# One f32 stack of two experts in place of two split ones, and a weight ring that grows once the dense experts are done

## The chip, the cores and the metric

The kernel runs on one core of a Trainium2 chip. The metric is device time in microseconds (us), lower is better. One execution is profiled; the times that follow from several runs are given beside it.

## The reference

A decoder layer for 256 tokens of width 2048: a token mixer (latent attention and an mLSTM, merged by gates), and then a mixture of 32 experts of width 512. Each token picks one group of eight experts and two experts in it. Only the second part is touched by the change:

```python
g_sel = jnp.argmax(g_logits, axis=-1)                      # one group of 4
top_p, top_i = lax.top_k(jax.nn.softmax(e_in, axis=-1), TOP_K)   # two experts of its 8
weights = g_w[:, None] * top_p / jnp.sum(top_p, axis=-1, keepdims=True)
comb = jnp.sum(jax.nn.one_hot(expert_idx, N_EXPERTS) * weights[..., None], axis=1)
...
hg = jnp.einsum('td,edf->tef', t, w_gate_e[sl])
hu = jnp.einsum('td,edf->tef', t, w_up_e[sl])
act = jax.nn.silu(hg) * hu * comb[:, sl, None]
out = out + jnp.einsum('tef,efd->td', act, w_down_e[sl])
```

An expert's weights are 12 MiB in f32. The reference multiplies every expert with every token and weights most products by zero; the kernel needs only the tokens that chose an expert. The reference's router, evaluated on the drawn inputs (seed 0), gives expert 0 133 tokens, and the others, sorted, 139, 50, 23, 19, 19, 17, 16, 13 and fewer; five experts get none.

## The kernel before

Up to about 780 us the kernel runs the mixer. From there on it runs the experts, and the rest of this text is about them.

**Units of work.** A router on the chip counts the tokens of each expert and ranks the experts by it. Expert 0 is taken out (`static`) and computed as a *dense* expert, for all 256 tokens, without waiting for the router; so is rank 0 (`HEAVY`). Ranks 1 and 2 are a *stack of one* each (`("stack", 1, 1)`): up to 128 tokens are gathered into the columns of one operand. Ranks 3 to 26 are six *stacks of four* (`LIGHT`): 32 columns each, so that four experts' tokens lie side by side in the 128 columns. Ranks 27 to 30 (`LAST`) run only if rank 27 has tokens. An expert with more tokens than its columns hold (`cap`, L1186 to L1188) goes through a loop at the end (`spill`) as a dense expert.

**Precision and cost.** Dense experts and stacks of one split each weight slab of 1 MiB into two parts, `whi` and `wlo` (`split`: ScalarE copies, VectorE subtracts), and multiply three times in fp32r (`mm3`, `mm_wide`). Stacks of four use the f32 slab as it lies in the ring (L1298, L1346), four matmuls of 32 columns for each 128 rows of weights, each on its own quarter of TensorE's columns.

**Buffers.** 1 MiB buffers come from two pools: `u8` (9) and `v8` (4, two of which hold the token rows `xr`). A ring of `RING = 7` of the `u8` serves the stacks of four (`fetch_used`, which skips the load of a rank without tokens); the `v8` two serve the split experts (`fetch`, "rawb" in the trace). `split` has three `whi` and three `wlo` of half that size (`W4 = 3`).

**What sets the order.** SyncE issues every load, in the order of the program. A load into the ring waits until TensorE has read what lay there; a load into a `v8` buffer waits until VectorE has split what lay there; whatever stands behind a waiting load waits too. The program itself is written by two generators, `heavy` and `light`, that are asked in turn: the one whose share of its total is behind goes next (`done[0] / total[0] > done[1] / total[1]`). A dense slab half counts 0.5, a chunk of a stack (one slab of each of its experts) counts its number of experts. `HEAVY_RATE = 1.8` sets the heavy total, 86.4 against 288 for the light one. On TensorE, ScalarE and VectorE a scheduler then orders the instructions, and each engine runs them strictly in that order.

Of the kernel before, what the change touches and what calls it, by code (L numbers as in the profile page):

```python
# [9 lines left out]
F32 = mybir.dt.float32  # L10
F32R = mybir.dt.float32r
# [7 lines left out]
P = 128  # L19
# [19 lines left out]
HTURN = [1, 1]  # L39
HEAVY_RATE = 1.8  # L40
W4 = 3
# [25 lines left out]
DENSE = 0  # L67
HEAVY = [("dense", 0), ("stack", 1, 1), ("stack", 2, 1)]
LIGHT = [("stack", r, 4) for r in (3, 7, 11, 15, 19, 23)]
LAST = ("stack", 27, 4)  # L70
# [3 lines left out]
def decoder_layer_kernel(ctx, tc, xT, c, pos, cols_d, const_d, mask_d, w_ada, w_head, w_half, w_blk, w_mlv, w_pa, w_pb, w_out,  # L74
# [14 lines left out]
    def u8(name, dt=F32):  # L89
        return big.tile([P, 2048], dt, name=name, tag="u8")  # L90

    def flat(x):
# [786 lines left out]

    def load_expert(e, w, ch, rank=None):  # L880
# [3 lines left out]
        src = w[bass.ds(e, 1), ch].rearrange("a p k -> p (a k)")  # L884
        return fetch(src) if rank is None else fetch_used(src, rank)

# [155 lines left out]
    def s2(name, dt=F32):  # L1042
        return b2.tile([P, 512], dt, name=name, tag="t2b")
# [45 lines left out]
    def router():  # L1089
# [132 lines left out]

    def halves(raw):
        return [split(raw[:, i * 1024:(i + 1) * 1024]) for i in range(2)]

    def prep(r0, E, heavy):
        C = P // E
# [17 lines left out]
        vec.tensor_scalar(gT[:, :T], cb[:, :T], 0.0, None, op0=ALU.is_gt)  # L1245
        xg = [u8("xg")] if E > 1 else [[], []]
        for q in range(4):
            b = bank("xb")
            for i in range(4):
                k = 4 * q + i  # L1250
                for tt in range(2):
                    pe.matmul(b[:, i * P:(i + 1) * P], xr[tt][:, k * P:(k + 1) * P], gt[tt], start=tt == 0, stop=tt == 1)  # L1252
            dst = xg[0][:, q * 512:(q + 1) * 512] if E > 1 else s2("xf")
# [6 lines left out]
            if E == 1:  # L1260
                hi, lo = tx("xh", "txh", F32R)[:, :512], tx("xl", "txl", F32R)[:, :512]
                act.activation(hi, dst, AF.Copy)
                vec.tensor_tensor(lo, dst, hi.bitcast(F32), op=ALU.subtract)
                xg[0].append(hi)
                xg[1].append(lo)
        return xg, gT, wc

    def mm_wide(out, xh, xl, wh, wl, first, last):
        pe.matmul(out, xh, wh, start=first, stop=False)
        pe.matmul(out, xl, wh, start=False, stop=False)  # L1270
        pe.matmul(out, xh, wl, start=False, stop=last)

    pre = {}

    def stack(r0, E, last):
# [4 lines left out]

        def gu_chunks():
            for m in range(8):
                ch = 4 * (m % 2) + m // 2
                raws = [load_expert(expert(n), w_gu, ch, n if E > 1 else None) for n in ranks]
                for a in range(2):
                    yield ch // 4, 4 * (ch % 4) + 2 * a, ([split(raws[0][:, a * 1024:(a + 1) * 1024])] if E == 1 else
                                                          [r[:, a * 1024:(a + 1) * 1024] for r in raws])

        for u, k0, ws in ahead1(gu_chunks()) if E == 1 else gu_chunks():
            for k in (k0, k0 + 1):  # L1290
                us = slice((k - k0) * 512, (k - k0 + 1) * 512)
                if E == 1:
                    ks = slice((k % 4) * P, (k % 4 + 1) * P)
                    mm_wide(gu[u], xg[0][k // 4][:, ks], xg[1][k // 4][:, ks], ws[0][0][:, us], ws[0][1][:, us],
                            k == 0, k == KT - 1)
                else:
                    for j in range(E):
                        pe.matmul(gu[u][j * C:(j + 1) * C, :], xg[0][:, k * P + j * C:k * P + (j + 1) * C], ws[j][:, us],  # L1298
                                  start=k == 0, stop=k == KT - 1)
            yield 0.5 * E  # L1300
        s = s2("s")
# [4 lines left out]
        for f in range(4):  # L1306
            pe.transpose(ab[:, f * P:(f + 1) * P], s[:, f * P:(f + 1) * P], ident)
        aT = [s2("aT", F32 if E > 1 else F32R) for _ in range(1 if E > 1 else 2)]
        act.activation(aT[0], ab, AF.Copy)
        if E == 1:  # L1310
            vec.tensor_tensor(aT[1], ab, aT[0].bitcast(F32), op=ALU.subtract)

        def dn_chunks():
            for ch in range(4):
                raws = [load_expert(expert(n), w_dn, ch, n if E > 1 else None) for n in ranks]
                yield ch, ([halves(raws[0])] if E == 1 else raws)

# [17 lines left out]
        done = None  # L1335
        for ch, ws in dn_chunks():
            yb = bank("yb")
            for f in range(4):
                fs = slice(f * P, (f + 1) * P)
                if E == 1:  # L1340
                    wh, wl = ws[0][f // 2]
                    o = slice((f % 2) * 512, (f % 2 + 1) * 512)
                    mm_wide(yb, aT[0][:, fs], aT[1][:, fs], wh[:, o], wl[:, o], f == 0, f == 3)
                else:
                    for j in range(E):
                        pe.matmul(yb[j * C:(j + 1) * C, :], aT[0][:, f * P + j * C:f * P + (j + 1) * C],  # L1346
                                  ws[j][:, f * 512:(f + 1) * 512], start=f == 0, stop=f == 3)
# [23 lines left out]


    def unit(u):
# [5 lines left out]
    def stream(units, gen=None):  # L1379
        heavy = gen is not None  # L1380
        ready = lambda u: u[0] == "dense" or u[1] in pre
        for i in range(-1 if gen else 0, len(units)):
            if i >= 0:
                if not ready(units[i]):
                    pre[units[i][1]] = prep(*units[i][1:], heavy)
                gen = unit(units[i])
            for what in gen:
                if what != "act":
                    yield what
                else:  # L1390
                    if i + 1 < len(units) and not ready(units[i + 1]):
                        pre[units[i + 1][1]] = prep(*units[i + 1][1:], heavy)
# [175 lines left out]
```

## Time and profile before

| | us |
|---|---|
| median of 3 runs (lowest to highest) | 1686.77 (1675.19 to 1690.32) |
| the profiled execution | 1683.75 |
| its span in the trace | 1682.0 |
| TensorE busy in the span | 1501.5 (89%) |
| VectorE, ScalarE busy | 895.5, 562.3 |
| bytes moved, mean rate | 561.02 MB, 334 GB/s |
| mean granted clock | 0.963 |

The share of busy time is a mean over stages with different limits, so the views by stretch are the ones to read: which engine is busy throughout, and at what rate the loads run beside it. A matmul's duration in the trace is longer than the distance to the next one, since they are pipelined; the distance between two starts is its cost. An f32 matmul is two records, so a row of "x2" is one of them. The trace's "idle before" names what ended a wait.

### The profile page before, as it was taken

The page shows a single profiled execution, that of the slowest core. Times are in us where ns is not written, and L with a number is a line of the kernel's source. Part 1 is how long each engine was busy: PE and PEld are TensorE (multiplying, and loading weights), DVE is VectorE, ACT ScalarE, POOL GpSimd, SP SyncE. Part 2 cuts the span into 40 slices and gives each one's busy share as a digit, 9 for nine tenths or more (in the row PEclk, how much of TensorE's full clock was granted, in tenths as well). Part 3 has the DMA queues.
Part 4 walks back from the last instruction along what each step waited for, and adds up shares of the span by engine and source line. Part 5 has one row for each costly group of instructions (what it writes and reads, how often), then busy time and mean ns, then how long its engine had stood idle before and what let it go on. Part 6 is the DMA issues. An engine that isn't in the chain of part 4 may idle for free.

```text
span 1682.0 us, 25284 instructions
## 1 busy us (share of the span) xinstructions
PE 1501.5 (89%) x9924; PEld 1071.2 (64%) x9924; DVE 895.5 (53%) x1272; ACT 562.3 (33%) x790; POOL 88.0 (5%) x91
## 2 busy tenths in 40 slices
PE   8799999999999999999978999988988887768775
PEld 5698997999999999999636565644443333113212
DVE  5877799888776789976313334444443421102102
ACT  3134665446645664444303122222322211001000
POOL 0140013000000000220000000000000000000000
PEclk9899999999999999999989999999999989999989
DMA  8978668888676789864679889779999999999997
GB/s 344 395 286 327 260 234 292 317 286 289 245 259 240 269 339 375 329 254 160 262 316 388 343 368 389 308 322 421 412 421 393 403 416 397 406 410 385 405 388 287
DMA packets 78467, 561.02 MB, mean 334 GB/s; under 512 B 8705, under 2 KB 8961, under 8 KB 11905
## 3 DMA queue, kind: packets, MB, share of 16 engines
q1 hardware_dynamic: 78050, 558.84, 84.3%
q8 instruction: 82, 1.34, 0.3%
q10 hardware_dynamic: 288, 0.45, 0.1%
q14 instruction: 47, 0.39, 0.1%
HBM read 569.74 MB, written 2.10 MB: 340 GB/s over the span
## 4 chain that ended last, share of the span: by engine, by line
PE 69%; DMA 18%; DVE 7%; ACT 3%; issue 2%; POOL 0%; SPq 0%; DVEq 0%; POOLq 0%; ACTq 0%
PE gu L1298 12%; DMA ring<-in_w_gu_dram 10%; DMA ring<-in_w_dn_dram 6%; PE yb L1346 5%; PE ga L196 4%; PE ga L198 4%; PE xb L1252 3%; PE ga L197 3%; DVE wlo L184 2%; DVE raw L140 2%; PE hp L198 2%; PE hp L196 2%; PE hp L197 2%; PE gu L196 2%; PE gu L198 2%
## 5 line engine op out<-in xcount | busy, mean ns | idle before, releaser
L1298 PE MATMUL gu<-ring,xg 128*32 128x512 f32 x1536 | 295.0, 672 | 74.1 <-DMA ring<-in_w_gu_dram 74.1
L183 ACT ACTIVATE whi<-raw 128x1024 fp32r<-128x1024 f32 (+1 forms) x222 | 229.8, 1039 | 272.5 <-PE ga L197 82.0
L184 DVE TENSOR_TENSOR wlo<-raw,whi 128x1024 fp32r<-128x1024 f32 (+1 forms) x222 | 267.4, 1211 | 85.0 <-ACT whi L183 83.3
L140 DVE SCALAR_TENSOR_TENSOR raw<-raw,cond 128x2048 f32<-128x2048 f32 x96 | 220.0, 2294 | 19.5 <-DMA raw<-in_w_ada_dram 19.4
L1298 PEld LDWEIGHTS gu<-ring,xg 128*32 128x32 f32 x1536 | 61.6, 120 | 248.2 <-DMA ring<-in_w_gu_dram 131.9
L184 DVE TENSOR_TENSOR wlo<-rawb,whi 128x1024 fp32r<-128x1024 f32 x84 | 99.5, 1222 | 131.4 <-ACT whi L183 131.4
L1346 PE MATMUL yb<-ring,aT 128*32 128x512 f32 x768 | 130.8, 604 | 21.7 <-DMA ring<-in_w_dn_dram 18.9
L196 PE MATMUL ga<-hh,whi 128*128 128x256 f32 x512 | 149.9, 293 | 0.0
L198 PE MATMUL ga<-hh,wlo 128*128 128x256 f32 x512 | 145.3, 284 | 0.8 <-DVE wlo L184 0.8
L197 PE MATMUL ga<-hl,whi 128*128 128x256 f32 x512 | 145.1, 283 | 0.0
L183 ACT ACTIVATE whi<-rawb 128x1024 fp32r<-128x1024 f32 x84 | 84.7, 1050 | 118.7 <-DMA rawb<-in_w_dn_dram 43.9
L1321 DVE TENSOR_TENSOR yl<-yb,yh 128x512 fp32r<-128x512 f32 x32 | 22.1, 690 | 155.4 <-ACT yh L1320 155.4
L196 PEld LDWEIGHTS ga<-hh,whi 128*128 128x128 f32 x512 | 98.0, 191 | 5.2 <-issue 3.8
L1320 ACT ACTIVATE yh<-yb 128x512 fp32r<-128x512 f32 x32 | 19.1, 597 | 242.9 <-PE yb L1346 216.0
L198 PEld LDWEIGHTS ga<-hh,wlo 128*128 128x128 f32 x512 | 98.0, 191 | 1.3 <-DVE wlo L184 1.2
L197 PEld LDWEIGHTS ga<-hl,whi 128*128 128x128 f32 x512 | 98.1, 192 | 0.8 <-issue 0.7
L198 PE MATMUL hp<-hh,wlo 128*128 128x256 f32 x320 | 91.8, 287 | 3.4 <-DVE wlo L184 3.2
L196 PE MATMUL hp<-hh,whi 128*128 128x256 f32 x320 | 92.8, 290 | 0.0
L197 PE MATMUL hp<-hl,whi 128*128 128x256 f32 x320 | 91.2, 285 | 0.0
L1346 PEld LDWEIGHTS yb<-ring,aT 128*32 128x32 f32 x768 | 29.5, 110 | 92.4 <-issue 46.7
L1302 ACT ACTIVATE s<-gu 128x512 f32<-128x512 f32 x8 | 4.8, 596 | 216.7 <-PE gu L1298 212.5
L196 PE MATMUL gu<-xgh,whi 128*128 128x258 f32 x256 | 73.8, 292 | 3.3 <-ACT whi L183 3.3
(435 smaller groups left out, 3105.8 us busy)
## 6 DMA issues: line engine op xcount, KB each, us to landing
ring<-in_w_gu_dram SPq DMA_DIRECT2D x192, 1024.0 KB, 10.1
raw<-in_w_ada_dram SPq DMA_DIRECT2D x96, 1024.0 KB, 6.7
ring<-in_w_dn_dram SPq DMA_DIRECT2D x96, 1024.0 KB, 10.4
raw<-in_w_blk_dram SPq DMA_DIRECT2D x32, 1024.0 KB, 5.0
rawb<-in_w_gu_dram SPq DMA_DIRECT2D x26, 1024.0 KB, 8.8
raw<-in_w_half_dram SPq DMA_DIRECT2D x20, 1024.0 KB, 6.3
raw<-in_w_out_dram SPq DMA_DIRECT2D x16, 1024.0 KB, 6.0
rawb<-in_w_dn_dram SPq DMA_DIRECT2D x16, 1024.0 KB, 9.4
```

Source lines behind the costliest of these rows:

```text
L140: vec.scalar_tensor_tensor(raw, raw, 1.0, cond, op0=ALU.mult, op1=ALU.mult, accum_out=mod[:, i:i + 1])
L183: keep(act.activation(hi, raw, AF.Copy))
L184: keep(vec.tensor_tensor(lo, raw, hi.bitcast(F32), op=ALU.subtract))
L196: pe.matmul(out, wh, xh, start=first, stop=False)
L197: pe.matmul(out, wh, xl, start=False, stop=False)
L198: pe.matmul(out, wl, xh, start=False, stop=last)
L1252: pe.matmul(b[:, i * P:(i + 1) * P], xr[tt][:, k * P:(k + 1) * P], gt[tt], start=tt == 0, stop=tt == 1)
L1298: pe.matmul(gu[u][j * C:(j + 1) * C, :], xg[0][:, k * P + j * C:k * P + (j + 1) * C], ws[j][:, us], start=k == 0, stop=k == KT - 1)
L1302: act.activation(s, gu[0], AF.Silu)
L1320: act.activation(yh, yb, AF.Copy)
L1321: vec.tensor_tensor(yl, yb, yh.bitcast(F32), op=ALU.subtract)
L1346: pe.matmul(yb[j * C:(j + 1) * C, :], aT[0][:, f * P + j * C:f * P + (j + 1) * C], ws[j][:, f * 512:(f + 1) * 512], start=f == 0, stop=f == 3)
```

## The change

Four things change.

1. Ranks 1 and 2 leave `HEAVY` and become one stack of two, the first unit of `LIGHT`: 64 columns for each expert, f32 slabs from the ring, two matmuls for each 128 rows of weights, nothing split. `cap` follows: 64 tokens for ranks 1 and 2. The code for stacks of one is gone.
2. The heavy total becomes `HEAVY_SHARE = 0.2` of the light total: 62.4 against 312.
3. The first group of matmuls of each chunk is kept together: the matmul of the last expert is issued first and the others after it (`together`), so no matmul of a chunk runs before the chunk's last slab has landed.
4. `whi` and `wlo` become halves of one 1 MiB tile (`w8`, three of them). When the heavy stream is through, the ring takes over two `v8` and three `w8`, one per chunk, and has 12 buffers.

```diff
-HEAVY_RATE = 1.8
+HEAVY_SHARE = 0.2
...
-HEAVY = [("dense", 0), ("stack", 1, 1), ("stack", 2, 1)]
-LIGHT = [("stack", r, 4) for r in (3, 7, 11, 15, 19, 23)]
+HEAVY = [("dense", 0)]
+LIGHT = [("stack", 1, 2)] + [("stack", r, 4) for r in (3, 7, 11, 15, 19, 23)]
...
-        hi = w4.tile([P, 1024], F32R, name="whi", tag="whi")[:, :n]
-        lo = w4.tile([P, 1024], F32R, name="wlo", tag="wlo")[:, :n]
+        both = w8("whl", F32R)
+        hi, lo = both[:, :n], both[:, 1024:1024 + n]
...
+    room = [u8] * RING
+
     def fetch_used(src, rank):
-        if len(ring) < RING:
-            ring.append(u8("ring"))
+        if room:
+            ring.append(room.pop(0)("ring"))
             nc.sync.dma_start(ring[-1], src)
             return ring[-1]
...
-        vec.tensor_scalar(cap, rank, 3.0, 96.0, op0=ALU.is_lt, op1=ALU.mult)
-        vec.tensor_scalar(over[:, 1:2], rank, 1.0, 128.0, op0=ALU.is_lt, op1=ALU.mult)
+        vec.tensor_scalar(cap, rank, 3.0, 32.0, op0=ALU.is_lt, op1=ALU.mult)
+        vec.tensor_scalar(over[:, 1:2], rank, 1.0, 192.0, op0=ALU.is_lt, op1=ALU.mult)
...
+    def together(calls):
+        head = calls[-1]()
+        with tc.issue_after(head.ins):
+            for call in calls[:-1]:
+                call()
...
+        def packed(out, x, k, ws, cut, first, stop):
+            def one(j):
+                return lambda: pe.matmul(out[j * C:(j + 1) * C, :], x[:, k * P + j * C:k * P + (j + 1) * C], ws[j][:, cut],
+                                         start=first, stop=stop)
+            return [one(j) for j in range(E)]
+
+        for m in range(8):
+            ch = 4 * (m % 2) + m // 2
+            u, k0 = ch // 4, 4 * (ch % 4)
+            ws = [fetch_used(expert_slab(n, w_gu, ch), n) for n in ranks]
...
+            together(calls[0])
+            for group in calls[1:]:
+                for call in group:
+                    call()
+            yield E
...
-    n_heavy, n_light = 12.0 * (1 + sum(u[2] if len(u) > 2 else 1 for u in HEAVY)) * HEAVY_RATE, 12.0 * sum(u[2] for u in LIGHT)
+    n_light = 12.0 * sum(u[2] for u in LIGHT)
+    n_heavy = HEAVY_SHARE * n_light
...
-    forced = []
+    forced, later = [], [v8] * 2 + [w8] * W4
...
             done[i] += got
+            if not streams[0] and later:
+                room.append(later.pop(0))
```

How it moves instructions shows at two places. The first is TensorE's order where the first chunk of the first stack meets the dense expert (`gu_7597` to `gu_7599` before, `gu_7387` to `gu_7389` now, are the dense expert's banks; `ring_...` is a slab of a stack). Before, a single matmul of the chunk stands between dense ones:

```order
L197 MATMUL gu_7597<-xgl_7234,whi_8051 128x258
L1298 MATMUL gu_7901<-ring_7912,xg_7848 32x512
L198 MATMUL gu_7597<-xgh_7233,wlo_8052 128x258
L196 MATMUL gu_7598<-xgh_7233,whi_8051 128x258
L197 MATMUL gu_7598<-xgl_7234,whi_8051 128x258
L198 MATMUL gu_7598<-xgh_7233,wlo_8052 128x258
```

Now the whole chunk stands in one piece:

```order
L199 MATMUL gu_7389<-xgh_7175,whl_7884 128x258
L1285 MATMUL gu_7688<-ring_7710,xg_7635 64x512
L1285 MATMUL gu_7688<-ring_7699,xg_7635 64x512 x2
L1285 MATMUL gu_7688<-ring_7710,xg_7635 64x512
L1285 MATMUL gu_7688<-ring_7699,xg_7635 64x512
...
L200 MATMUL gu_7389<-xgl_7176,whl_7884 128x258
```

Of the chunks of four, the order before has 55 such single matmuls between other work before its last split matmul; now a chunk of four is 16 rows without a break, throughout. Behind the router the order now reads, from the last gather of the first stack on (d: rows of a dense expert, c2 and c4: a chunk of the stack of two or of four): 31 d, c2, 23 d, c2, 15 d, five c2, 8 rows of the next gather, c2, 24 of the gather, the turn to the down weights, two c2, 25 d, c2, c2, 23 and 63 d, c4, 74 d, c4, 7 d, two c4, 48 d, c4, 48 d, c4, 48 d, two c4, and from there c4 and 48 d in turn, with a gather of 32 rows at each stack's end. The last dense rows stand ahead of the last down chunk of the second stack of four (ranks 7 to 10).

The second place is SyncE's order in the third stack of four, where the ring grows. Before, at a like place, each load into the ring is the next of the seven:

```order
L1064 DMA ring_7995<-in_w_gu_dram 128x2048
L1064 ISA
L1064 REGISTER_ALU
L1064 ISA
L1064 DMA ring_7912<-in_w_gu_dram 128x2048
```

Now a new buffer (`ring_10460`, one of the `v8`) comes in between, and four more follow, one in each of the next chunks:

```order
L1074 DMA ring_7732<-in_w_gu_dram 128x2048
L1071 ISA
L1071 DMA ring_10460<-in_w_gu_dram 128x2048
L1074 ISA
L1074 REGISTER_ALU
L1074 ISA
L1074 DMA ring_7734<-in_w_gu_dram 128x2048
```

Further up in the same order, the 24 loads of the stack of two and the first 16 of the next stack now stand ahead of the first load of a dense expert's down slab; before, 28 loads of a stack stood there.

## Rows read from the trace of the kernel before

**Rows 1.** The profile's page, part 2: granted clock and load rate in 40 slices.

```profile
PEclk9899999999999999999989999999999989999989
...
GB/s 344 395 286 327 260 234 292 317 286 289 245 259 240 269 339 375 329 254 160 262 316 388 343 368 389 308 322 421 412 421 393 403 416 397 406 410 385 405 388 287
```

**Rows 2.** Stretches: length, busy of PE, PEld, DVE, ACT, POOL, clock, DMA share, GB/s.

```profile
812.00:880.00 68.00, 59.29 (x381) 31.41 (x382) 15.60 (x28) 11.52 (x19) 0.00 (x0) 0.92 0.80 319
880.00:1140.00 260.00, 237.13 (x1614) 151.97 (x1609) 100.37 (x169) 63.96 (x95) 0.00 (x0) 0.98 0.87 353
1140.00:1320.00 180.00, 159.04 (x831) 77.37 (x830) 73.68 (x117) 48.01 (x66) 0.00 (x0) 0.96 0.99 409
1320.00:1665.00 345.00, 258.97 (x1449) 88.23 (x1447) 60.63 (x125) 28.36 (x46) 0.00 (x0) 0.93 0.98 403
1665.00:1682.00 17.00, 5.11 (x36) 1.99 (x36) 2.47 (x6) 0.60 (x1) 0.00 (x0) 0.78 0.25 96
...
812.00:1665.00 853.00, 714.44 (x4265) 348.98 (x4264) 250.27 (x437) 151.84 (x225) 0.00 (x0) 0.95 0.93 383
```

**Rows 3.** Three stretches of 20 us, columns as in rows 2.

```profile
860.00:880.00 20.00, 12.65 (x60) 2.92 (x62) 1.89 (x7) 0.05 (x1) 0.00 (x0) 0.74 0.97 396
1140.00:1160.00 20.00, 17.78 (x86) 9.08 (x86) 9.25 (x14) 3.75 (x5) 0.00 (x0) 1.00 1.02 422
1520.00:1540.00 20.00, 17.66 (x122) 9.74 (x118) 4.79 (x11) 4.85 (x10) 0.00 (x0) 0.98 0.86 342
```

**Rows 4.** Loads by destination: count, size, median us from issue to landing.

```profile
ring<-in_w_gu_dram SPq DMA_DIRECT2D x192, 1024.0 KB, 10.1
...
ring<-in_w_dn_dram SPq DMA_DIRECT2D x96, 1024.0 KB, 10.4
...
rawb<-in_w_gu_dram SPq DMA_DIRECT2D x26, 1024.0 KB, 8.8
...
rawb<-in_w_dn_dram SPq DMA_DIRECT2D x16, 1024.0 KB, 9.4
```

**Rows 5.** Timeline of SyncE's queue: start, length, line, what it issued.

```profile
786.27 24.38 SPq L1061 DMA_DIRECT2D ring<-in_w_gu_dram  x7
814.77 65.75 SPq L1064 DMA_DIRECT2D ring<-in_w_gu_dram  x21
```

**Rows 6.** PE's timeline, first stack's first chunk: start, length, line, tiles.

```profile
793.28 7.09 PE L1252 MATMUL xb<-G,xr 128*128 128x128 f32 x62
...
800.42 1.05 PE L1298 MATMUL gu<-ring,xg 128*32 128x512 f32 x2
801.39 0.39 PE L198 MATMUL gu<-xgh,wlo 128*128 128x258 f32 x1
...
802.10 0.28 PE L197 MATMUL gu<-xgl,whi 128*128 128x258 f32 x1
802.22 0.28 PE L198 MATMUL gu<-xgh,wlo 128*128 128x258 f32 x1
...
811.96 3.63 PE L1298 MATMUL gu<-ring,xg 128*32 128x512 f32 x28
815.51 0.39 PE L196 MATMUL gu<-xgh,whi 128*128 128x258 f32 x1
```

**Rows 7.** Timeline of PE: the pace of one expert's split matmuls.

```profile
1186.94 0.39 PE L1269 MATMUL gu<-whi,xh 128*128 128x512 f32 x1
1187.17 0.39 PE L1270 MATMUL gu<-whi,xl 128*128 128x512 f32 x1
```

**Rows 8.** The chain that ended last, in the tail: start, length, what.

```profile
1424.73 2.81 PE yb L1346 x24
1427.55 7.10 DMA ring<-in_w_dn_dram
```

**Rows 9.** SyncE's own waits, 790 to 1682 us: us in total, times, longest.

```profile
SPq L1064 <- PE gu L1298: 391.3, 57, 14.5
...
SPq L1053 <- DVE wlo L184: 38.9, 13, 7.0
```

More of the change, by code (lines that the diff above doesn't have):

```diff
@@ L90, in u8, with w8 @@
         return big.tile([P, 2048], dt, name=name, tag="u8")
+    def w8(name, dt=F32):
+        return w4.tile([P, 2048], dt, name=name, tag="w8")
     def flat(x):
@@ L878, in decoder_layer_kernel, with slab, expert_slab, load_expert @@
             proj(i - GATE_AHEAD)
-    def load_expert(e, w, ch, rank=None):
+    def slab(e, w, ch):
+        return w[bass.ds(e, 1), ch].rearrange("a p k -> p (a k)")
+    def expert_slab(r, w, ch):
+        return slab(expert(r), w, ch)
+    def load_expert(e, w, ch):
         if isinstance(e, int):
@@ L883, in load_expert @@
             return ahead[n] if n < len(ahead) else fetch(w[e, ch])
-        src = w[bass.ds(e, 1), ch].rearrange("a p k -> p (a k)")
-        return fetch(src) if rank is None else fetch_used(src, rank)
+        return fetch(slab(e, w, ch))
     def ahead1(gen):
@@ L1221, in accumulate, with prep @@
         vec.scalar_tensor_tensor(xs[:, d], src, mod[:, 80 + d:81 + d], xs[:, d], op0=ALU.mult, op1=ALU.add)
-    def halves(raw):
-        return [split(raw[:, i * 1024:(i + 1) * 1024]) for i in range(2)]
-    def prep(r0, E, heavy):
+    def prep(r0, E):
         C = P // E
@@ L1245, in prep @@
         vec.tensor_scalar(gT[:, :T], cb[:, :T], 0.0, None, op0=ALU.is_gt)
-        xg = [u8("xg")] if E > 1 else [[], []]
+        xg = u8("xg")
         for q in range(4):
@@ L1252, in prep @@
                     pe.matmul(b[:, i * P:(i + 1) * P], xr[tt][:, k * P:(k + 1) * P], gt[tt], start=tt == 0, stop=tt == 1)
-            dst = xg[0][:, q * 512:(q + 1) * 512] if E > 1 else s2("xf")
+            dst = xg[:, q * 512:(q + 1) * 512]
             for i in range(4):
@@ L1259, in prep @@
                     act.activation(dst[:, ks], b[:, ks], AF.Identity, bias=mod[:, 48 + k:49 + k], scale=gs[:, 1, k:k + 1])
[L1260 to L1265, printed above, removed]
         return xg, gT, wc
[L1268 to L1271, printed above, removed]
     pre = {}
+    def together(calls):
[3 more added lines that the diff above has]
+                call()
     def stack(r0, E, last):
@@ L1279, in stack @@
         gu = [bank("gu") for _ in range(2)]
[L1281 to L1300, printed above, removed]
+        def packed(out, x, k, ws, cut, first, stop):
[7 more added lines that the diff above has]
+            ws = [fetch_used(expert_slab(n, w_gu, ch), n) for n in ranks]
+            calls = []
+            for i in range(4):
+                k = k0 + i
+                calls.append(packed(gu[u], xg, k, ws, slice(i * 512, (i + 1) * 512), k == 0, k == KT - 1))
+            together(calls[0])
[3 more added lines that the diff above has]
+            yield E
         s = s2("s")
@@ L1307, in stack @@
             pe.transpose(ab[:, f * P:(f + 1) * P], s[:, f * P:(f + 1) * P], ident)
[L1308 to L1316, printed above, removed]
+        aT = s2("aT")
+        act.activation(aT, ab, AF.Copy)
         def finish(ch, yb):
@@ L1335, in stack @@
         done = None
-        for ch, ws in dn_chunks():
+        for ch in range(4):
+            ws = [fetch_used(expert_slab(n, w_dn, ch), n) for n in ranks]
             yb = bank("yb")
[L1338 to L1347, printed above, removed]
+            calls = [packed(yb, aT, f, ws, slice(f * 512, (f + 1) * 512), f == 0, f == 3) for f in range(4)]
+            together(calls[0])
+            for group in calls[1:]:
+                for call in group:
+                    call()
             if done:
@@ L1379, in stream @@
     def stream(units, gen=None):
-        heavy = gen is not None
         ready = lambda u: u[0] == "dense" or u[1] in pre
@@ L1384, in stream @@
                 if not ready(units[i]):
-                    pre[units[i][1]] = prep(*units[i][1:], heavy)
+                    pre[units[i][1]] = prep(*units[i][1:])
                 gen = unit(units[i])
@@ L1391, in stream @@
                     if i + 1 < len(units) and not ready(units[i + 1]):
-                        pre[units[i + 1][1]] = prep(*units[i + 1][1:], heavy)
+                        pre[units[i + 1][1]] = prep(*units[i + 1][1:])
                     yield "act"
     heavy, light = stream(HEAVY, first), stream(LIGHT)
-    n_heavy, n_light = 12.0 * (1 + sum(u[2] if len(u) > 2 else 1 for u in HEAVY)) * HEAVY_RATE, 12.0 * sum(u[2] for u in LIGHT)
+    n_light = 12.0 * sum(u[2] for u in LIGHT)
+    n_heavy = HEAVY_SHARE * n_light
     streams, total, done = [heavy, light], (n_heavy, n_light), [started, 0.0]
-    forced = []
+    forced, later = [], [v8] * 2 + [w8] * W4
     while any(streams):
```

## The prediction

> **What bounds the kernel now.** I read the page's slices first [rows 1]: from slice 20 on (about 800 us) the load rate is 160 to 390 GB/s at first and about 400 later. The reader is to see two regimes. Then the stretches [rows 2]: from 812 us, shortly before the first load waits for a ring buffer [rows 5], to 1665 us, when the last slab has landed, the rate is 383 GB/s over 853 us, so 326.7 MB, or 312 slabs of 1.049 MB. Single stretches hold 422 [rows 3]. At that rate a slab takes 2.48 us and the 326.7 MB take 774 us; the loads therefore stand still for 853 - 774 = 79 us. By stretch that is 68 x (1 - 319/422) = 17 us up to 880, 260 x (1 - 353/422) = 43 up to 1140, 5 up to 1320, 16 in the tail [rows 2]. In the first two TensorE is busy 59 of 68 and 237 of 260 us, so it sets the pace and loads wait for buffers (SyncE's longest wait is for the stacks' matmuls, 391 us in 57 waits [rows 9]); in the tail the chain alternates between a load and three of a chunk's four groups, 7.10 + 2.81 = 9.9 us for four slabs, which is the load rate itself [rows 8].
>
> So the bytes are the floor. The change moves the same bytes: 24 slabs of ranks 1 and 2 go through the ring instead of the split buffers [rows 4]. It can win at most the 79 us, and it wins what it takes off TensorE while TensorE sets the pace.
>
> **Part by part.** *The stack of two.* Removed: two experts of 48 x 3 = 144 split matmuls each, 0.23 us apart [rows 7]: 66 us of TensorE, 48 splits on ScalarE and VectorE, and one gather of 7.1 us [rows 6]. Added: 12 chunks of four groups. A chunk of four runs its last 13 matmuls in 815.51 - 811.96 = 3.55 us [rows 6], four column tiles side by side. No row shows 64-column tiles. If two of them overlap as the four do, a chunk costs 3.6 us, 43 us in all; if not, its eight matmuls cost the 0.97 us of a lone one each (800.42 to the next start at 801.39 [rows 6]), 7.8 us a chunk, 93 in all. I take 3.6, the nearer row, as the matmuls are the same but for the number of columns. Against the 73 us removed this saves 30 us.
>
> *Chunks in one piece.* Before, up to three matmuls of a chunk run alone between dense ones, about 0.97 us each, and then 3.55 us: 6.5 us for a chunk; now 3.6. With 55 such matmuls before the split work ends, up to 50 us of TensorE go. The price is that TensorE waits at a chunk's first matmul for its last slab, with dense work queued behind; the cover is that the load, then, is what everything waits for, and the loads go on as long as buffers are free.
>
> *Heavy share, ring of 12, joined halves.* The dense rows move between chunks; a slab's 48 rows cost 48 x 0.12 = 5.8 us [rows 6]. The joined halves add no instruction; a copy may wait one matmul (0.12 us) longer for its buffer; I count nothing, since two other split buffers cover it. The loads' queue: 40 ring loads instead of 28 stand ahead of the first dense down slab; it is needed only after those chunks, so I count nothing for it.
>
> *The sum, by the loads.* Floor: 812 + 774 = 1586 us.
>
> Start: from 800 us, where the gather ends [rows 6], TensorE's order up to the first chunk of ranks 3 to 6 holds 180 dense rows (21.6 us), 12 chunks (43), a gather (7), 32 combining rows of the same width (3.8) and the turn from gate to down weights (about 3, from the gaps around it): 79 us, until 879. The loads of that time are the stack's other 17 slabs and the next seven, 24 x 2.48 = 60 us from 812, done at 872. Then they wait for the first chunk of four, over at 883, and once more 2.5 us before the second, behind 74 dense rows. That is 14 us lost. Bounds: 5 us, if the first fill runs later than I have it (seven issues spread over 24 us [rows 5]), and the 17 of before plus as much again.
>
> Dense stretch, to about 1150: a chunk of four and a dense slab take 5 x 2.48 = 12.4 us to load and 3.6 + 5.8 = 9.4 us of TensorE. When a chunk's last slab lands, three ring slabs and one dense slab, 9.9 us, are under way before a buffer must come free; TensorE is at worst at the start of a dense slab, 9.4 us from freeing one. The loads barely go on. Bounds: 0, and before's 353 of 422 GB/s kept up for 240 us, 39. I take the rate of 1140 to 1320, 409 [rows 2], where chunks met shorter split work, as here: 7 us.
>
> Tail, 180 slabs (four stacks of 48, less 12 of a rank without tokens): before's loss scaled to it is 16 x 447/345 = 20 us, most of it at a stack's turn, where the rate falls to 342 [rows 3]. With 12 buffers eight slabs (20 us) are ahead of the chunk in work instead of three (7.5). Bounds 0 and 20; I take 4, as a turn (a gather of 7 and a wait of about 3 us) is longer than 7.5 but not than 20.
>
> End: 17 us from the last slab, as before [rows 2].
>
> 1586 + 14 + 7 + 4 + 17 = 1628 us of span, and 1683.75 - 1682.0 = 1.75 around it: **1630 us**, 3.2% below the profiled execution, which itself is 0.2% below the median of its runs.
>
> **The rivals.** *A: the two 64-column tiles do not overlap.* 12 x 4.2 = 50 us more in the first stage, where TensorE sets the pace; less the 8 or so that the ring hides, 1630 + 42 = 1672. For it: no row shows this shape. Against it: the four narrower ones overlap. 7%. By the Trainium skill, "TensorEngine Tiling (Array Packing)", section Tiling Modes, the array without row tiling splits into two tiles of 64 columns or four of 32 that work independently; the sum is then the one above, and the trace of before can confirm only the four.
>
> *B: the loads keep stopping in the dense stretch.* 9.4 against 9.9 us is little room, and where TensorE waits for loads its granted clock falls: it is 0.74 in 860 to 880 us, with TensorE busy 12.7 of 20 us, and 1.00 in the stretches around [rows 3]. At 1.2 instead of 2.4 GHz the 9.4 us become 18.8. At before's rate: 1630 + 39 - 7 = 1662. Against it: the clock's mean is 0.96 from 1140 to 1320, with much waiting for loads [rows 2]. 14%.
>
> *C, slower: lockstep at the dense slabs.* SyncE's queue holds a dense slab's load until an earlier one is split (13 such waits, 38.9 us, 7.0 at most [rows 9]); the split waits for a joined buffer, and that for dense matmuls, which now stand behind a whole chunk that waits for the loads behind that very slab. Each dense slab caught so costs the chunk and the slab in series, 9.4 us. There are 16; from six on nothing is won, and ten give 1630 + 94 = 1724. Against it: two slab buffers and three halves are in turn, so a slab's load waits for work two slabs back. 4%.
>
> *D: the loads are at their limit already and nothing is won*, about 1684. Against it: 422 GB/s stand beside 383 in the same stage [rows 2, 3]. 1%. The Trainium skill, "SBUF — State Buffer", section Summary: rules for kernel authors, says to estimate HBM loads with about 358 GB/s; by it the 326.7 MB would need 913 us, more than the 853 they took. This case's 422 speaks against it and for "HBM Reference", section Specifications (TRN2), which gives about 425 for a core that streams alone.
>
> *E: spilled experts.* Ranks 1 and 2 hold 64 tokens each now; with 65 a dense pass more (12 x 5.8 = 70 us) follows. The reference's router gives 50 and 23. Under 1%.
>
> **The numbers.** Forecast 74%, its own range 1612 to 1650: the start between 5 and 25, the dense stretch 0 to 15, the tail 0 to 20. A 7%, B 14%, C 4%, D and E 1%. Runs of before differ by 0.9% from lowest to highest, so about 1% is what a measurement tells from no change. The range, 1608 to 1666, takes in B and leaves out A, C, D and E and the forecast's edges. Faster by over 1% (below about 1670): the forecast and two thirds of B, 83%. Within 1%: A, D and the rest of B, 13%. Slower: C and E, 4%.
>
> **What would show it.** Right: the span near 1628; no row of TensorE's split matmuls in stacks; chunks of two at about 3.6 us; a rate of 405 to 422 from 880 us on, near 422 at the stacks' turns, and an early dip around 875 us; the last dense matmul near 1150. A shows in chunks of two at 7 to 8 us. B shows in a rate near 350 with a lower clock between 900 and 1150, C in SyncE's waits for VectorE of over 100 us. The forecast is wrong if the loads, with buffers free, do not hold 422 for hundreds of us, or if the mixer's 780 us move with the joined halves.

## The result: 1641 us, and the profile after

The changed kernel takes 1641.2 us (median of 4 runs, 1636.3 to 1644.0) against 1686.4 of the kernel before; the ratio is 0.974 (95% interval 0.971 to 0.978). The profiled execution took 1639.2 us, its span is 1637.3. The forecast was 1630, with 1608 to 1666 as its range. The time came out near; the experiments show that three of the prices that the prediction set on the parts did not hold.

The page's slices, answering to [rows 1]: of the last row, the slices of the last quarter but the very last now stand at 420 to 422 GB/s, where before had 385 to 416.

```profile
PEclk9899999999999999999999889998868878888888
...
GB/s 383 374 283 329 282 212 283 327 286 296 245 273 242 269 267 416 321 297 155 224 409 273 416 400 378 420 417 393 399 421 422 420 422 421 420 422 421 421 421 228
```

The stretches, with the columns of [rows 2]; the last slab lands at 1618.6 us instead of 1665.4.

```profile
812.00:880.00 68.00, 63.27 (x373) 36.45 (x373) 21.15 (x45) 14.82 (x27) 0.00 (x0) 0.97 0.96 382
880.00:908.00 28.00, 24.78 (x196) 15.07 (x194) 8.73 (x16) 4.45 (x9) 0.00 (x0) 0.94 0.68 272
908.00:1150.00 242.00, 192.62 (x1484) 125.44 (x1478) 77.02 (x132) 47.37 (x71) 0.00 (x0) 0.90 0.98 400
1150.00:1618.00 468.00, 310.10 (x2008) 111.55 (x2006) 63.55 (x148) 27.61 (x51) 0.00 (x0) 0.82 1.01 418
...
812.00:1618.00 806.00, 590.76 (x4049) 288.50 (x4048) 170.44 (x340) 94.25 (x158) 0.00 (x0) 0.86 0.98 404
```

Against the 422 GB/s of [rows 3] the loads stand still for 68 x (1 - 382/422) = 6.4 us, then 10.0, 12.6 and 4.4: 33 us instead of before's 79. TensorE is busy 63 of 68 and 25 of 28 us up to 908, then 193 of 242 and 310 of 468, so from 908 on it no longer sets the pace. Two stretches of 20 us, answering to [rows 3]: a hole behind the stack of two, and a stack's turn that no longer shows.

```profile
880.00:900.00 20.00, 19.88 (x164) 13.80 (x162) 4.44 (x7) 2.89 (x7) 0.00 (x0) 1.00 0.55 216
...
1520.00:1540.00 20.00, 14.91 (x108) 5.97 (x104) 6.17 (x14) 1.20 (x2) 0.00 (x0) 0.87 1.01 421
```

The loads, answering to [rows 4]: 24 slabs moved to the ring, and a ring load now lands 15 us after its issue. With more buffers a load is issued further ahead: with seven, in experiment 1, the same loads land after 9.5 us.

```profile
ring<-in_w_gu_dram SPq DMA_DIRECT2D x208, 1024.0 KB, 14.8
ring<-in_w_dn_dram SPq DMA_DIRECT2D x104, 1024.0 KB, 15.1
...
rawb<-in_w_gu_dram SPq DMA_DIRECT2D x10, 1024.0 KB, 10.4
```

TensorE's chunks, answering to [rows 6] (start, duration, idle before): first a chunk of two and the first chunk of four, each right behind dense rows.

```profile
801.64 3.65 PE L1285 MATMUL gu<-ring,xg 128*64 128x512 f32 x16
805.22 0.39 PE L200 MATMUL gu<-xgl,whl 128*128 128x258 f32 x1
...
881.92 3.64 PE L1285 MATMUL gu<-ring,xg 128*32 128x512 f32 x32
```

The two 64-column tiles overlap: the next matmul starts 3.58 us after the chunk's first (801.64 to 805.22), as for four tiles. Then three chunks of the tail:

```profile
1446.93 5.22 PE L1285 MATMUL gu<-ring,xg 128*32 128x512 f32 x32 [4.87 <-DMA ring<-in_w_gu_dram]
1457.57 5.02 PE L1285 MATMUL gu<-ring,xg 128*32 128x512 f32 x32 [5.42 <-DMA ring<-in_w_gu_dram]
1467.53 5.17 PE L1285 MATMUL gu<-ring,xg 128*32 128x512 f32 x32 [4.93 <-DMA ring<-in_w_gu_dram]
```

These chunks in one piece wait 5 us for their last slab and then run 5.0 to 5.2 us, not 3.6; from 1440 to 1480 us the granted clock is 0.84, a mix of the two levels. Two stretches take it apart, one in the first of these chunks and one over a chunk of 3.64 us (from 1368.07) that follows a gather without a wait; the columns are those of [rows 2]:

```profile
1447.00:1450.00 3.00, 3.00 (x16) 0.72 (x20) 0.00 (x0) 0.00 (x0) 0.00 (x0) 0.50 1.01 421
...
1368.00:1371.60 3.60, 3.60 (x34) 0.94 (x32) 1.05 (x3) 0.91 (x2) 0.00 (x0) 1.00 1.02 423
```

After its wait the chunk starts at 0.50, the level of 1.2 GHz; the chunk without a wait has 1.00, the level of 2.4 GHz, throughout. This is what the prediction did not see. The last stack, from about 1540 us, is an exception to the chunks in one piece: one of its ranks has no tokens, so no load, and there single matmuls still run ahead of the rest (at 1548.42 and 1563.32, for example).

### The profile page after: what moved, and what is told of

It is laid out like the page before. It is cut to its first block, busy times and chain, and to the rows that moved or that the text cites. A ratio compares the mean times of both kernels' runs of the same rounds, so it can differ in the third digit from the quotient of the medians.

```text
span 1637.3 us, 24656 instructions
## 1 busy us (share of the span) xinstructions
PE 1378.5 (84%) x9726; PEld 1009.6 (62%) x9726; DVE 815.3 (50%) x1177; ACT 504.2 (31%) x720; POOL 87.4 (5%) x91
## 4 chain that ended last, share of the span: by engine, by line
PE 50%; DMA 33%; DVE 6%; ACT 3%; issue 2%; POOL 1%; SPq 0%; DVEq 0%; POOLq 0%; ACTq 0%
DMA ring<-in_w_gu_dram 22%; DMA ring<-in_w_dn_dram 11%; PE gu L1285 6%; PE ga L199 4%; PE yb L1285 4%; PE ga L201 3%; PE ga L200 3%; DVE whl L187 2%; PE hp L201 2%; PE hp L199 2%; PE hp L200 2%; PE xb L1259 2%; PE wo L199 1%; DVE raw L143 1%; PE wo L201 1%
## 5 line engine op out<-in xcount | busy, mean ns | idle before, releaser
L1285 PE MATMUL gu<-ring,xg 128*32 128x512 f32 (+1 forms) x1664 | 270.4, 756 | 138.0 <-DMA ring<-in_w_gu_dram 138.0
L187 DVE TENSOR_TENSOR whl<-raw,whl 128x1024 fp32r<-128x1024 f32 (+1 forms) x222 | 267.1, 1210 | 93.1 <-ACT whl L186 92.6
L186 ACT ACTIVATE whl<-raw 128x1024 fp32r<-128x1024 f32 (+1 forms) x222 | 229.5, 1038 | 255.3 <-PE ga L201 62.7
L143 DVE SCALAR_TENSOR_TENSOR raw<-raw,cond 128x2048 f32<-128x2048 f32 x96 | 220.3, 2296 | 16.5 <-DMA raw<-in_w_ada_dram 16.4
L1285 PE MATMUL yb<-ring,aT 128*32 128x512 f32 (+1 forms) x832 | 130.7, 725 | 64.0 <-DMA ring<-in_w_dn_dram 61.9
L199 PE MATMUL ga<-hh,whl 128*128 128x256 f32 x512 | 149.6, 292 | 0.0
L201 PE MATMUL ga<-hh,whl 128*128 128x256 f32 x512 | 145.0, 283 | 1.4 <-DVE whl L187 1.3
L200 PE MATMUL ga<-hl,whl 128*128 128x256 f32 x512 | 144.8, 283 | 0.0
L199 PEld LDWEIGHTS ga<-hh,whl 128*128 128x128 f32 x512 | 97.9, 191 | 5.1 <-issue 3.5
L201 PEld LDWEIGHTS ga<-hh,whl 128*128 128x128 f32 x512 | 97.9, 191 | 2.0 <-DVE whl L187 2.0
L200 PEld LDWEIGHTS ga<-hl,whl 128*128 128x128 f32 x512 | 98.0, 191 | 1.0 <-issue 0.7
L201 PE MATMUL hp<-hh,whl 128*128 128x256 f32 x320 | 91.7, 287 | 3.4 <-DVE whl L187 3.3
L199 PE MATMUL hp<-hh,whl 128*128 128x256 f32 x320 | 92.6, 290 | 0.0
L200 PE MATMUL hp<-hl,whl 128*128 128x256 f32 x320 | 91.2, 285 | 0.0
```

The source lines that it names most:

```text
L143: vec.scalar_tensor_tensor(raw, raw, 1.0, cond, op0=ALU.mult, op1=ALU.mult, accum_out=mod[:, i:i + 1])
L199: pe.matmul(out, wh, xh, start=first, stop=False)
L200: pe.matmul(out, wh, xl, start=False, stop=False)
L201: pe.matmul(out, wl, xh, start=False, stop=last)
L1285: return lambda: pe.matmul(out[j * C:(j + 1) * C, :], x[:, k * P + j * C:k * P + (j + 1) * C], ws[j][:, cut], start=first, stop=stop)
```

## The experiments

Ratios are to the kernel before, whose median was 1681 to 1684 us in these sessions.

**1. The ring stays at seven.**

```diff
-    forced, later = [], [v8] * 2 + [w8] * W4
+    forced, later = [], []
```

> The changed kernel with a ring that stays at seven buffers. Theory (the ring's growth pays in the tail): the tail's rate falls back from the 418 GB/s of the changed kernel's 1150 to 1618 us to before's 403, with single stretches of 20 us near 342 at the stacks' turns; 468 us x (418/403 - 1) = 17 us, so about 1656 us. Rival (with each chunk in one piece seven buffers are enough): the turns stay at 420 GB/s and the time at about 1641.

Measured: 1686.4 us, 1.002 (1.000 to 1.004): the theory's direction at far more than its size, and not the rival. All of the gain is gone: the ring's growth is worth 45 us, not 17. The columns are those of the stretches; nearly all of the change is in the tail, at 379 GB/s, lower than before's 403.

```profile
908.00:1150.00 242.00, 191.76 (x1498) 126.14 (x1499) 77.14 (x132) 47.29 (x71) 0.00 (x0) 0.92 0.98 401
...
1250.00:1600.00 350.00, 210.76 (x1312) 71.55 (x1311) 41.91 (x100) 18.97 (x37) 0.00 (x0) 0.80 0.95 379
```

The chain of work that ended last, in the tail of this kernel (start, length, what):

```profile
1450.38 5.75 PE gu L1285 x32
1456.13 4.80 DMA ring<-in_w_gu_dram
...
1460.97 5.36 PE gu L1285 x32
1466.33 5.36 DMA ring<-in_w_gu_dram
```

A whole chunk and then a load stand in series, 10.6 and 10.8 us for four slabs, where 422 GB/s need 9.9; from 1150 to 1540 us chunks start 10.0 to 12.4 us apart, 11.1 in the mean. When a chunk's last slab lands, three more are under way (7.5 us). The chunk frees its buffers near its end, 5.4 to 5.8 us later, and a load issued then lands only about 5 us after that. In the changed kernel the chain from 1437 to 1477 us is loads alone.

**2. Plain order, ring of twelve.**

```diff
-        head = calls[-1]()
-        with tc.issue_after(head.ins):
-            for call in calls[:-1]:
-                call()
+        for call in calls:
+            call()
```

> The changed kernel with the first group of a chunk in plain program order, so that its matmuls may run one by one before the chunk's last slab has landed. Theory (lone matmuls cost TensorE up to 50 us where it sets the pace): the dense stretch (908 to 1150 us in the changed kernel, TensorE busy 193 of 242 us) fills up and the last dense matmul comes 10 to 25 us later, so 1651 to 1666 us; the tail keeps 418 GB/s. Rival (the loads set the pace there by now, so TensorE has room for the lone matmuls): about 1641, with only TensorE's busy time up.

Measured: 1660.0 us, 0.987 (0.984 to 0.990), as the theory had it; the last dense matmul comes at 1188 us instead of 1165. Its stretches:

```profile
880.00:908.00 28.00, 28.00 (x184) 17.10 (x184) 7.32 (x11) 3.77 (x8) 0.00 (x0) 1.00 0.44 174
908.00:1150.00 242.00, 218.45 (x1424) 127.98 (x1420) 73.99 (x128) 45.49 (x70) 0.00 (x0) 0.96 0.94 387
1150.00:1250.00 100.00, 78.31 (x436) 29.40 (x438) 19.69 (x40) 6.17 (x8) 0.00 (x0) 0.90 0.95 392
1250.00:1600.00 350.00, 255.59 (x1476) 84.68 (x1468) 44.95 (x105) 21.74 (x42) 0.00 (x0) 0.94 1.01 421
```

The 19 us are lost before 1250 us: where the changed kernel loads 272 GB/s, this one loads 174, with TensorE busy throughout. TensorE is busy 1459.5 us in all against 1378.5, 81 us more; 29 of them lie between 880 and 1150 us, most of the others in the tail, where it has time to spare. From 1250 us on the order makes no difference to the rate.

**3. Both edits: plain order, ring of seven.** The two diffs above together.

> The changed kernel with both edits at once: seven ring buffers throughout, and the first group of a chunk in plain order. Theory (a chunk in one piece lets TensorE wait 5 us and then run at about half clock, 5.0 to 5.3 us instead of 3.6, and only then frees four of seven buffers; matmuls issued as the slabs land keep it at 3.6): the tail goes from the 381 GB/s of seven buffers in one piece back to 400 or more, so 1660 of the loose order plus 468 x (415/402 - 1) = 15 us, about 1675, below the 1686 of one piece with seven buffers. Rival (seven buffers are too few in either order): 381 GB/s in the tail, 1660 + 468 x (415/381 - 1) = about 1702.

Measured: 1680.2 us, 0.998 (0.996 to 1.000), near the theory and far from the rival. The tail:

```profile
1250.00:1600.00 350.00, 251.22 (x1422) 81.54 (x1422) 44.97 (x105) 21.72 (x42) 0.00 (x0) 0.94 0.98 403
```

And a chunk in it, between 1310 and 1320 us:

```profile
1311.50 1.05 PE L1283 MATMUL yb<-ring,aT 128*32 128x512 f32 x2
1313.00 1.05 PE L1283 MATMUL yb<-ring,aT 128*32 128x512 f32 x2 [0.46 <-DMA ring<-in_w_dn_dram]
1315.50 3.62 PE L1283 MATMUL yb<-ring,aT 128*32 128x512 f32 x26 [1.45 <-DMA ring<-in_w_dn_dram]
```

The single matmuls run while TensorE would wait; the last piece then takes 3.6 us, in a tail with a clock of 0.94. In the chain of this kernel three of the chunk's four groups stand ahead of the next load, 2.81 + 7.08 = 9.9 us (from 1315.50), as in [rows 8]: the buffers come free 2.8 us behind the last slab and not 5.4. So, in us:

| | seven buffers | growing to twelve | the growth |
|---|---|---|---|
| chunks in plain order | 1680 | 1660 | -20 |
| chunks in one piece | 1686 | 1641 | -45 |
| one piece instead of plain | +6 | -19 | |

**4. A ring that grows to nine.**

```diff
-    forced, later = [], [v8] * 2 + [w8] * W4
+    forced, later = [], [v8] * 2
```

> The changed kernel with a ring that grows to nine buffers (by the two of the dense slabs alone) instead of twelve. Theory (what counts is the load time of the buffers beyond the four of the chunk in work): five beyond it are 5 x 2.49 = 12.4 us, enough for a chunk of 5.3 us between loads, so 421 GB/s between the stacks' turns, and not enough for a turn (a gather of 7 us, a chunk and a wait of 3 us), which loses 3 to 5 us at eight or nine turns: 1641 + 25 to 40 us at the most, about 1660. Rival (each chunk loses a part of what it loses with seven, in proportion): 1686 - 2/5 x 45 = 1668, with a rate near 397 all along the tail.

Measured: 1642.7 us, 0.976 (0.973 to 0.979); the changed kernel's time. The theory was right between the stacks' turns and wrong at them, the rival wrong throughout: two buffers do nearly all the work of five. The tail's stretch, and TensorE at a turn:

```profile
1250.00:1600.00 350.00, 225.86 (x1444) 77.31 (x1436) 42.45 (x100) 19.36 (x38) 0.00 (x0) 0.81 1.01 417
...
1358.89 6.55 PE L1285 MATMUL gu<-ring,xg 128*32 128x512 f32 x32 [3.55 <-DMA ring<-in_w_gu_dram]
...
1371.10 3.64 PE L1285 MATMUL gu<-ring,xg 128*32 128x512 f32 x32
1374.67 2.05 PE L1259 MATMUL xb<-G,xr 128*128 128x128 f32 x16
...
1379.59 3.64 PE L1285 MATMUL yb<-ring,aT 128*32 128x512 f32 x32 [2.44 <-DMA ring<-in_w_dn_dram]
```

The theory put a gather of 7 us, a chunk and a wait of 3 us, 15 us in all, between two times at which buffers come free. TensorE's order has a chunk inside the gather, so three chunks end at 1365.4, 1374.7 and 1383.2 us, 9.3 and 8.5 us apart; that is less than the 12.4 us of five slabs, and the rate from 1360 to 1380 us is 419 GB/s.

**5. The stack of two alone.** The kernel before with:

```diff
-HEAVY = [("dense", 0), ("stack", 1, 1), ("stack", 2, 1)]
-LIGHT = [("stack", r, 4) for r in (3, 7, 11, 15, 19, 23)]
+HEAVY = [("dense", 0)]
+LIGHT = [("stack", 1, 2)] + [("stack", r, 4) for r in (3, 7, 11, 15, 19, 23)]
...
+    n_light = 12.0 * sum(u[2] for u in LIGHT)
+    n_heavy = 0.3 * n_light
```

> The kernel before with the stack of two alone: ranks 1 and 2 as the first light unit, heavy total 0.3 of the light one (the ratio of before), lone matmuls, separate split halves and seven ring buffers as before. Theory (the terms of the prediction add up): TensorE loses 30 us of work where it sets the pace, and the tail stays at 403 GB/s, so 1686 - 30 = about 1656 us. Rival 1 (the lone matmuls and the short ring keep the loads waiting anyway): above 1670. Rival 2 (the stack alone takes TensorE off the path and the rest adds nothing but the tail's 17 us): 1641 + 17 = 1658 and a dense stretch at 400 GB/s; it differs from the first in the rate there, which would be 353 to 380 under the first.

Measured: 1699.5 us, 1.011 (1.007 to 1.014): above 1670, as rival 1 had it, but slower than before, which none had. The page's part 1 for this kernel says that the work did go:

```profile
PE 1476.2 (87%) x9726; PEld 1022.3 (60%) x9726; DVE 816.8 (48%) x1177; ACT 504.6 (30%) x720; POOL 89.0 (5%) x91
```

TensorE is busy 25 us less than before, and the loads are slower all the same. In the stretches of [rows 2] they were 319, 353, 409 and 403 GB/s; now:

```profile
812.00:880.00 68.00, 68.00 (x368) 37.59 (x366) 17.81 (x33) 15.37 (x28) 0.00 (x0) 1.00 0.76 298
880.00:1140.00 260.00, 230.11 (x1553) 141.48 (x1553) 88.40 (x154) 47.95 (x71) 0.00 (x0) 0.97 0.88 353
1140.00:1320.00 180.00, 130.29 (x731) 44.69 (x724) 24.14 (x57) 13.29 (x26) 0.00 (x0) 0.91 0.96 392
1320.00:1665.00 345.00, 245.95 (x1352) 73.70 (x1350) 38.68 (x91) 17.48 (x33) 0.00 (x0) 0.92 0.97 397
```

At the start TensorE is busy for all of the 68 us, with dense rows between the chunks of two. From 1140 us on the rate is lower by 6 to 17 GB/s, though TensorE has 50 of 180 us to spare up to 1320. My reading is that before, the split experts' slabs had two buffers of their own there beside the seven of the ring, and that now every slab goes through the seven.

**6. The same, with less dense work between its chunks.**

```diff
-    n_heavy = 0.3 * n_light
+    n_heavy = 0.2 * n_light
```

> The kernel before with the stack of two, as in the run that had it alone, but the heavy total at 0.2 of the light one instead of 0.3: nothing of the change is then missing but the chunks in one piece, the joined split halves and the ring's growth. Theory (the pace of the dense work is what the stack alone lacked: 81 dense rows stood between its chunks while the loads waited): as the loose order with seven buffers, 1680. Rival (the joined halves or another detail made up those 19 us): about 1699.

Measured: 1683.0 us, 1.001 (0.998 to 1.004), as the theory had it: the time of experiment 3 within the intervals. So against the kernel before the stack at this pace of dense work is worth nothing, at 0.3 it costs 16 us, and the joined halves add nothing measurable. The kernel before with its split stacks at a slower pace was not run.

**7. Everything but the stack of two.** The kernel before, its stacks of one and its heavy ratio kept, with the diffs of the chunks in one piece, of the joined halves and of the ring's growth.

```diff
+    forced, later = [], [v8] * 2 + [w8] * W4
...
+                if E > 1:
+                    yield ch // 4, 4 * (ch % 4), raws
+                    continue
...
+                    group([lambda j=j, k=k, us=us: pe.matmul(
+                        gu[u][j * C:(j + 1) * C, :], xg[0][:, k * P + j * C:k * P + (j + 1) * C], ws[j][:, us],
+                        start=k == 0, stop=k == KT - 1) for j in range(E)], k == k0)
```

> The kernel before with its two split stacks of one and its heavy ratio kept, and all else of the change: chunks of four in one piece, joined split halves, and the ring's growth once the heavy work is through (which now leaves only two full stacks of four behind it). Theory (terms add up): it lacks the stack's 30 us, so 1641 + 30 = about 1671 us, with a dense stretch near 370 GB/s. Rival 1 (chunks in one piece free enough of TensorE by themselves): below 1655, with 400 GB/s in the dense stretch. Rival 2 (without the stack of two the chunk in one piece makes the loads wait behind TensorE's wait): 1686 or more.

Measured: 1627.6 us, 0.967 (0.965 to 0.970): 14 us faster than the change with its stack of two; rival 1. Two of its stretches:

```profile
880.00:908.00 28.00, 25.97 (x211) 21.77 (x212) 14.20 (x30) 8.73 (x14) 0.00 (x0) 0.94 1.01 419
908.00:1150.00 242.00, 208.71 (x1597) 146.13 (x1595) 104.42 (x178) 66.59 (x97) 0.00 (x0) 0.96 0.97 399
```

The hole behind 880 us is not there, 28 x (419 - 272)/422 = 10 us. Two things could fill it: that no stack of two stands at the start, or the pace of the dense work. The next three runs tell them apart.

**8. The change at another pace of dense work.** `HEAVY_SHARE` 0.2 becomes 0.3, then 0.13.

> The changed kernel with the heavy total at 0.3 of the light one instead of 0.2, the ratio that the kernel with split stacks and all else of the change had. Theory (that kernel's 1628 come from where its units stand, not from its pace of dense work): no gain here, 1641 or up to 10 us more, since 80 more dense rows (10 us of TensorE) stand between the chunks of the stack of two, while the loads wait. Rival (the pace of dense work makes the difference): 1628 to 1633.

Measured: 1636.8 us, 0.972 (0.969 to 0.976), not to be told from the changed kernel's 0.974 and above the rival's 1628 to 1633. The hole is smaller and the stretch ahead of it slower, 340 GB/s instead of 382: the loss moves.

```profile
812.00:880.00 68.00, 68.00 (x415) 40.45 (x411) 20.10 (x38) 16.10 (x28) 0.00 (x0) 1.00 0.88 340
880.00:908.00 28.00, 24.98 (x193) 18.73 (x192) 17.69 (x32) 8.01 (x13) 0.00 (x0) 0.94 0.91 375
```

> The changed kernel with the heavy total at 0.13 of the light one. Theory (dense rows between the first chunks hold up the loads): 25 dense rows and a dense down half leave the stretch before the first chunks of four, the hole at 880 to 908 us (272 GB/s, 10 us lost) shrinks by a half, and the dense work lasts one stack longer while the loads keep to 400 GB/s: 1630 to 1638. Rival (the ring, which grows a stack later, is worth more): the third stack of four runs at 381 to 400 GB/s instead of 418, 100 us x (418/390 - 1) = 7 us, about 1645 to 1650.

Measured: 1648.1 us, 0.980 (0.977 to 0.984); the rival. The start is better, and more than that is lost later, where the ring has not yet grown:

```profile
812.00:880.00 68.00, 54.36 (x309) 25.49 (x307) 17.57 (x42) 11.86 (x24) 0.00 (x0) 0.98 0.99 401
880.00:908.00 28.00, 26.33 (x201) 18.39 (x205) 5.49 (x5) 5.30 (x5) 0.00 (x0) 0.87 0.93 371
908.00:1150.00 242.00, 179.82 (x1315) 103.38 (x1307) 59.99 (x116) 33.31 (x55) 0.00 (x0) 0.87 0.96 386
1150.00:1250.00 100.00, 73.06 (x539) 41.80 (x542) 25.09 (x50) 16.84 (x29) 0.00 (x0) 0.87 0.99 408
```

**9. The stack of two last.**

```diff
-LIGHT = [("stack", 1, 2)] + [("stack", r, 4) for r in (3, 7, 11, 15, 19, 23)]
+LIGHT = [("stack", r, 4) for r in (3, 7, 11, 15, 19, 23)] + [("stack", 1, 2)]
```

> The changed kernel with the stack of two as the last of the light units instead of the first, all else the same. Theory (at the start its twelve chunks of 3.6 us stand against 5 us of loads each, with dense rows and two gathers between them, so TensorE sets the pace and the ring lies full; in the tail nothing else is there to do): the hole at 880 to 908 us goes, the tail stays at 418 GB/s, about 1628 to 1633. Rival 1 (the stack costs nothing at the start): 1641. Rival 2 (a chunk of two at half clock, about 5.2 us against 5.0 us of loads, holds the loads up at the end, where twelve chunks and two turns lose 1 to 2 us each): 1645 to 1655.

Measured: 1627.9 us, 0.968 (0.964 to 0.971), as the theory had it, and its 1624.6 to 1631.6 lie clear of the changed kernel's 1636.3 to 1644.0. Its stretches:

```profile
880.00:908.00 28.00, 18.56 (x138) 8.08 (x137) 6.19 (x11) 5.93 (x12) 0.00 (x0) 0.88 0.98 403
908.00:1150.00 242.00, 194.42 (x1514) 131.33 (x1512) 87.87 (x157) 45.41 (x65) 0.00 (x0) 0.92 1.00 411
...
1250.00:1600.00 350.00, 244.80 (x1540) 89.57 (x1542) 47.45 (x112) 23.79 (x46) 0.00 (x0) 0.87 1.00 417
```

At the end the same stack runs where TensorE has time to spare (245 of 350 us busy) and costs nothing: the time is that of experiment 7, which has the split stacks. So it is the place that cost 13 us.

**10. Combining ahead of the next chunk.** In experiment 9's kernel `if done: combine(*done)` moves ahead of the chunk's matmuls; then `HEAVY_SHARE` 0.3 besides.

> The kernel with the stack of two last, and with the combining matmuls of a down chunk ahead of the next chunk's matmuls instead of behind them. Theory (behind the last slab the last chunk's result waits for the previous chunk's combining, 8 matmuls and an addition of 1.7 us; ahead, they run while TensorE waits for slabs): 2 us less at the end, about 1626. Rival (the combining waits for ScalarE and VectorE, with the chunk behind it, and the buffers come free later): 2 to 10 us more, 1630 to 1638.

Measured: 1628.6 us, 0.967 (0.964 to 0.970), no difference that can be told. The end is shorter, as the theory says: from the last chunk's first matmul to the first that needs its `yl` 5.1 us pass instead of 6.7. It is too little to show in the whole.

> The same, with the heavy total at 0.3 of the light one. Theory (from 908 to 1150 us the loads ran at 411 GB/s, and the ring grows two thirds of a stack earlier): the dense stretch stays at 400 to 411 and the tail at 421, between 1620 and 1627. Rival (with more dense rows to a chunk TensorE sets the pace from 880 to 1080 us): 390 GB/s there, 200 us x (411/390 - 1) = 11 us more, about 1637.

Measured: 1625.9 us, 0.966 (0.963 to 0.969), as the theory had it, and the fastest of all by its median, though its interval overlaps that of experiment 9. Its stretches from 880 us on hold 408 to 421 GB/s.

## Why the time was right, and which steps were not

**The bytes as the floor: right.** The 326 MB from 812 us on were moved at 404 GB/s, with 420 to 422 for hundreds of us in the tail. By the Trainium skill, "HBM Reference", section Specifications (TRN2), a core that streams alone gets about 425 GB/s; the 421 over 350 us of experiment 2 agrees.

**The sum by stretches: right to 9 us.** Start 16.4 us lost instead of 14 (6.4 + 10.0; the hole stood at 880 to 900, foretold around 875, and was deeper than the 405 GB/s that the prediction asked for from 880 on: 272 up to 908); dense stretch 12.6 instead of 7, at 400 GB/s, with the last dense matmul at 1165 instead of 1150; tail 4.4 instead of 4; end 1637.3 - 1618.6 = 18.7 instead of 17, since the previous chunk's combining now stands behind the last chunk: from the last slab's landing to the first matmul that needs the last `yl` 6.6 us pass (1618.64 to 1625.28); before, with the combining ahead, it was 5.1 (1665.45 to 1670.52), as in experiment 10. Together that is 10 us, and the span missed 1628 by 9.

**What each part brings: wrong in three steps.** The sum by stretches did not add these prices up, so it could come out without them.

- *"Against the 73 us removed this saves 30 us."* The price of a chunk was right (3.58 us against 3.6), and so nearly was the work (25 us less of TensorE, experiment 5). That it turns into time was wrong: alone it is worth 0 (experiment 6) or costs 16 us (5), and with all the rest it costs 13 at the place where it stands (7, 9). Where TensorE set the pace, at the start, the stack put 43 us of chunks and a gather in front of the first stack of four; the split work it removed lay later, beside loads that had buffers of their own.
- *"6.5 us for a chunk; now 3.6"*, and the cover for its wait. The "up to 50 us" of TensorE's work, up to the end of the split work, came to 29 between 880 and 1150 us (81 in all, experiment 2). And behind a wait of 3 to 7 us most chunks take 4.9 to 6.6 us, at the lower clock for a part of it; with seven buffers the next load stands behind all of that: +6 us. Only with the longer ring is it worth its 19.
- *"before's loss scaled to it is 16 x 447/345 = 20 us."* That is about what the growth is worth to chunks in plain order (20 us, experiments 2 and 3; the intervals allow some 6 us either way). The bound was taken from a kernel whose chunks ran as slabs landed, and used for one whose chunks run in one piece; there it is 45. Nor are twelve buffers needed: nine do (4), since at a turn buffers come free 9.3 and 8.5 us apart, and not only behind a gather of 7, a wait of about 3 and a chunk.

**Edits counted at nothing.** The joined halves: right (6). The pace of the dense work: right for chunks in one piece (1637 against 1641), not at 0.13, where some 7 us are lost (1648, experiment 8), and wrong for plain order, where 0.3 and 0.2 lie 16 us apart (5, 6).

**The rivals.** A fell with the chunk of two at 3.58 us. B was partly there: the clock fell to 0.90 in the dense stretch and its loss is 12.6 us, within the forecast's own bound of 15 and far from the 39. (Its reading of the clock was loose: [rows 3] has 1.00 and 0.98 far from 860 to 880 us; next to it stand 1.00 before and 0.91 behind.) C did not come: SyncE's waits for VectorE's splits are 22.8 us from 790 us on, two waits, where C would show in over 100. D fell with 421 GB/s in the tail. E did not come: no dense matmul follows 1165 us. The mixer did not get longer either: the first ring load is issued at 782.8 us, before at 786.3.

So the time was right because a load rate near 422 was the right thing to sum up to, and because what each stretch would still lose was read well from TensorE's order and the number of buffers. A part of it is luck. The tail's 4 us were reckoned with chunks of 3.6 us; twelve buffers happened to have room for chunks of 4.9 to 6.6 as well, where with seven the same slip costs 45 us. And the prices of the parts, 30 us for the stack and 16 (20 less 4) for the ring, were off in opposite directions: 0 or less, and 45.

Open: how the 6 to 17 GB/s that the tail of experiment 5 lost divide between buffers and order.

## What to carry to other kernels

- A bound taken from a profile holds for the shape of work it was read from: when two edits meet in one resource (here the order of a chunk and the number of buffers), price them together, or run the two-by-two.
- Work taken off an engine is worth time only in the stretch where that engine ends the wait; look at where the new work lands, and put it where the engine idles.
- When loads are the floor, count the slabs under way at the moment the last buffer of a group is still held; two more buffers were worth 44 us here, the next three nothing.

## What the runs showed of the hardware

The same 32 matmul records of a chunk take 3.6 us behind other work, at a granted clock of 1.00 (1368.07 in the changed kernel). Behind a wait of 3 to 7 us for a load most take 4.9 to 6.6 us (1150 to 1540 us, changed kernel and experiment 1); the one at 1446.93 starts at a clock of 0.50. Where single matmuls run during that wait, the rest mostly takes 3.6 us (experiments 2 and 3). From 1250 to 1600 us the mean granted clock is 0.94 with them and 0.80 to 0.83 without, 1 being the level of 2.4 GHz. The loads hold 421 GB/s at 0.94 (experiment 2) and at 0.83 (the changed kernel).
